# Every seventh chunk of expert weights multiplied whole as fp32

## The chip, the cores and the metric

The kernel runs on one core of one Trainium2 chip. The metric is the device time of one launch in microseconds (us). In the profile PE is TensorE's matmul, PEld its weight load, DVE is VectorE, ACT is ScalarE, POOL is GpSimd and SP is SyncE, which issues most DMAs.

## The reference

A block of 256 tokens of width 1024 goes through a mixer, a memory attention, a mixture of experts and then two further attention and feed-forward layers, all in fp32. The change lies in the mixture of experts, which is, cut to its core:

```
expert = grp * EXPERTS_PER_GROUP + top_i          # 2 of 32 experts for each of 256 tokens
def run_block(args):
    e, tok, w = args
    xb = xt[tok]
    hid = jax.nn.silu(xb @ w_gate[e]) * (xb @ w_up[e])     # 1024 x 512 each
    return (hid @ w_down[e]) * w[:, None].astype(xb.dtype) # 512 x 1024
```

All 32 experts' weights are read: 32 x 6 MB of fp32.

## The kernel before

Matmuls are done in fp32r, which keeps fewer bits of an fp32 number. To stay near fp32, each operand is split into a high half (the value rounded to fp32r) and a low half (what is left), and the halves' products are added up.

**The experts.** The 32 experts go in 16 units of two. Each expert's tokens sit in 32 slots. The stationary operand is built so that a 128-column slice of it (`xf[:, k0 + k, e * 64:e * 64 + P]`) holds the high and the low half of one expert's tokens, with zeros in the other expert's place, so one matmul with it gives high and low rows of the result at once; a small matmul with `comb` adds them up later.

**The chunks.** The weights come in chunks of 256 rows by 512 columns (128 partitions x 2 x 512, 512 KB), 12 for an expert, 384 in all. For each chunk in turn `stream` (L1021) does: one DMA on SP's queue into a raw buffer (`load`, L276); `high` (L286) on ACT, which writes the high half `wh`; `low` (L291) on DVE, which subtracts it from the raw chunk and writes the low half `wl` (for a few early chunks on POOL, `POOLED`); and `go` in `parts` (L1010), which issues four matmuls of 128x512 on PE: two row blocks of `wh`, then two of `wl`. Then `tick` runs whatever the agenda has due at this chunk: `clock[0]` is the number of chunks done. There are 4 buffers for `wh`, 4 for `wl`, and 27 places for raw chunks (`places`, `shared`), so ACT and DVE can be up to four chunks ahead of PE.

**The order.** Every instruction of this path is wrapped in `keep`, which fixes its order on its engine. Unit u runs `up(u)` (16 chunks for gate and up), then `down(u - 1)` (8 chunks). So chunk numbers run: up(0) 0 to 15, up(1) 16 to 31, down(0) 32 to 39, up(2) 40 to 55, and so on, 24 for each unit. Between chunks stand, by the agenda:
- `read` and `hidden` of `up` (L1067, L1072): after the third chunk of the following down, ACT copies the sums (L1068) and PE adds high and low rows with `comb` (L1070); after the fifth chunk, `hidden` runs a chain ACT sigmoid (L1078), DVE, DVE, ACT cast (L1082), DVE. ACT and DVE work in order, so the sixth chunk's `high` stands behind that chain.
- `scatter` (L1106), `gather` (L933) and `weights` (L1046): small fp32 matmuls and transposes; an fp32 matmul shows as two records in the trace.

The matmuls of `mm<-` are those of up, those of `at<-` are of down.

Of the kernel before, what the change touches and what calls it, by code (L numbers as in the profile page):

```python
# [13 lines left out]
F32 = mybir.dt.float32  # L14
# [6 lines left out]
P = 128  # L21
# [4 lines left out]
KC = 2  # L26
RAW = 4
MOE_RAW = 16
LAG = 3
POOLED = (4, 24, 3)  # L30
EARLY = 25
PAST = 16
OVER = 10
# [81 lines left out]
def forward(ctx: ExitStack, tc: tile.TileContext, a: dict, out: bass.AP):  # L115
    nc = tc.nc
    mm = nc.tensor.matmul
# [151 lines left out]
    def keep(ins):  # L269
        return tc.keep_in_program_order(ins)  # L270

    def chunk(pool, tag, kc, n, dt=F32):
        v = new(pool, [P, KC, 512], dt, name=tag, **({"bufs": 2} if tag == "Y" else {}))
        return v if n == 512 else v.rearrange("p k n -> p (k n)")[:, 0:kc * n].rearrange("p (k n) -> p k n", n=n)

    def load(parts, kc, n, pool=wraw, tag="raw"):  # L276

        raw = chunk(pool, tag, kc, n)
        at = 0
        for src in parts:  # L280
            w = src.shape[1]
            nc.sync.dma_start(out=raw[:, :kc, at:at + w], in_=src.rearrange("(k p) n -> p k n", p=P))
            at += w
        return raw

    def high(raw, kc, n, order=free):  # L286
        h = chunk(whi, "wh", kc, n, F32R)
        order(nc.scalar.activation(h[:, :kc], raw[:, :kc], AF.Copy))  # L288
        return h

    def low(raw, h, kc, n, order=free, eng=nc.vector):  # L291
        l = chunk(wlo, "wl", kc, n, F32R)
        order(eng.tensor_sub(l[:, :kc], raw[:, :kc], h[:, :kc].bitcast(F32)))  # L293
        return l
# [422 lines left out]
    def nextraw():  # L717

        return next(v for v in raws if not closing or v[0] is not big or v[1] in ("kTc", "vc"))
# [169 lines left out]
    last = len(UNITS) - 1  # L889
    xs2 = []  # L890
    for u in range(2):
        xs2.append(new(mp, [P, KD, 3, 2, 32], F32R, name="xs%d" % u))
        if u == 0:
            wt = s3("wt", 32)
            upcoming = [W[e, k0 * P:(k0 + KC) * P] for i in range(2) for e in UNITS[i] for W in (wg, wu) for k0 in range(0, KD, KC)]
            ahead.extend(load([src], KC, 512, *nextraw()) for src in upcoming[len(first):][:EARLY])
    hs2 = []
# [7 lines left out]
    agenda, clock = collections.defaultdict(list), [0]  # L905
# [7 lines left out]
    def tick():  # L913
        clock[0] += 1
        for fn, args in agenda.pop(clock[0], ()):
            fn(*args)
# [93 lines left out]
    def parts(xf, e, nk, last, acc, W, col):  # L1010

        def go(k0, ww):
            for i in range(2):
                for k in range(KC):
                    keep(mm(acc, xf[:, k0 + k, e * 64:e * 64 + P], ww[i][:, k],  # L1015
                            start=(e == 0 and k0 == 0 and i == 0 and k == 0),
                            stop=(e == last and k0 + KC == nk and i == 1 and k == KC - 1)))

        return [(W[k0 * P:(k0 + KC) * P, col:col + 512], functools.partial(go, k0)) for k0 in range(0, nk, KC)]

    def stream(chunks):  # L1021
        for src, go in chunks:
            if ready:
                go(ready.popleft())
            else:
                raw = ahead.popleft() if ahead else load([src], KC, 512, *nextraw())
                h = high(raw, KC, 512, keep)
                go((h, low(raw, h, KC, 512, keep, nc.gpsimd if clock[0] < POOLED[1] and clock[0] % POOLED[0] == POOLED[2] else nc.vector)))
            tick()

    def flat(v):
# [27 lines left out]
    def up(u):  # L1059

        G, U = new(psm, [P, 512], name="mm"), new(psm, [P, 512], name="mm")
        at(2 if u else PAST, weights, u)
        stream(up_chunks(u, G, U))
        gu = [new(tmp, [P, 512], name="rows") for _ in range(2)]
        ps = new(psm, [P, 2, 4, 64], name="mm")

        def read(i, v):  # L1067
            keep(nc.scalar.copy(gu[i], v))  # L1068
            for k in range(4):
                keep(mm(ps[:, i, k], gu[i][:, k * P:(k + 1) * P], comb, start=True, stop=True))  # L1070

        def hidden():  # L1072
            if u < 2:
                hs2.append(new(mp, [P, 4, 3, 2, 32], F32R, name="hs%d" % u))
                nc.gpsimd.memset(hs2[u][:, :, 1].bitcast(F32), 0.0)
            hs = hs2[u % 2]
            hid = new(mp2, [P, 4, 64], name="hid")
            keep(nc.scalar.activation(hid, ps[:, 0], AF.Sigmoid))  # L1078
            keep(nc.vector.tensor_mul(hid, hid, ps[:, 0]))
            keep(nc.vector.tensor_mul(hid, hid, ps[:, 1]))  # L1080
            hv = hid.rearrange("p k (e r) -> p k e r", e=2)
            keep(nc.scalar.copy(hs[:, :, 0::2, 0], hv))  # L1082
            keep(tt(hs[:, :, 0::2, 1], hv, hs[:, :, 0::2, 0].bitcast(F32), op=ALU.subtract))

        at(LAG - 4, read, 0, G)
        at(LAG, read, 1, U)
        at(LAG + 2, hidden)
# [5 lines left out]
    def down(u):  # L1093

        Y = [new(psa, [P, 512], name="at") for _ in range(2)]
        stream(down_chunks(u, Y))
        Yg[u] = new(mp, [P, 2, 512], name="Y", bufs=2)
        for half in range(2):
            at(LAG - 2 + 2 * half, lambda *v: keep(nc.scalar.copy(*v)), Yg[u][:, half], Y[half])
# [125 lines left out]
    for i, v in enumerate(both):  # L1225
        at(ADDS + i, add, *v, last - 1)
    chunks = down_chunks(last, Y)
    stream([chunks[i] for i in (0, 1, 4, 5, 2, 3, 6, 7)])
    flush()
    rows_out(0)  # L1230
# [323 lines left out]
```

## Time and profile before

| what | value |
|---|---|
| time, median of 3 runs | 1588.86 us (1588.35 to 1589.14) |
| the profiled execution's own time | 1591.64 us |
| its span | 1590.0 us |
| PE busy, share of the span | 1532.9 us, 96% |
| DVE busy | 1190.1 us, 75% |
| ACT busy | 992.1 us, 62% |
| mean granted TensorE clock | 0.989 of full |

The experts' chunks are multiplied from 296 us to 826 us of the span. The profiled execution is 2.8 us above the median of the timed runs, 1.64 us of its time lies outside the span. Busy time of PE counts modelled ends that overlap with the next matmul, so PE's load is better read from the distances between starts.

### The profile page before, as it was taken

The page shows a single profiled execution, that of the slowest core. Times are in us where ns is not written, and L with a number is a line of the kernel's source. Part 1 is how long each engine was busy: PE and PEld are TensorE (multiplying, and loading weights), DVE is VectorE, ACT ScalarE, POOL GpSimd, SP SyncE. Part 2 cuts the span into 40 slices and gives each one's busy share as a digit, 9 for nine tenths or more (in the row PEclk, how much of TensorE's full clock was granted, in tenths as well). Part 3 has the DMA queues.
Part 4 walks back from the last instruction along what each step waited for, and adds up shares of the span by engine and source line. Part 5 has one row for each costly group of instructions (what it writes and reads, how often), then busy time and mean ns, then how long its engine had stood idle before and what let it go on. Part 6 is the DMA issues. An engine that isn't in the chain of part 4 may idle for free. (4 is left out here: it accounts for less than half of the span.)

```text
span 1590.0 us, 20604 instructions
## 1 busy us (share of the span) xinstructions
PE 1532.9 (96%) x7099; PEld 1194.5 (75%) x7099; DVE 1190.1 (75%) x1498; ACT 992.1 (62%) x1353; POOL 199.8 (13%) x95
## 2 busy tenths in 40 slices
PE   7999999699999999999999999999999999999998
PEld 5778887466776767767667887888888887888886
DVE  5665575789999999999887876766656876766654
ACT  5455554579878887797774666555544566455543
POOL 1110000434335141142001000000000000000000
PEclk9999999899999999999999999999999999999999
DMA  8645559689999999999956545566567545566653
GB/s 283 218 137 160 182 173 375 209 295 370 386 387 387 386 387 340 341 386 386 387 187 195 147 141 164 182 189 186 185 186 220 168 137 152 178 195 186 184 187 106
DMA packets 220348, 383.59 MB, mean 241 GB/s; under 512 B 13464, under 2 KB 60000, under 8 KB 219856
## 3 DMA queue, kind: packets, MB, share of 16 engines
q1 hardware_dynamic: 217584, 373.76, 70.2%
q0 software_dynamic: 1648, 6.84, 1.4%
q10 hardware_dynamic: 1008, 1.64, 0.3%
q8 instruction: 57, 0.93, 0.2%
q14 instruction: 51, 0.42, 0.1%
HBM read 381.10 MB, written 2.65 MB: 241 GB/s over the span
## 5 line engine op out<-in xcount | busy, mean ns | idle before, releaser
L293 DVE TENSOR_TENSOR wl<-raw,wh 128x1024 fp32r<-128x1024 f32 x599 | 718.0, 1227 | 239.6 <-ACT wh L288 226.1
L288 ACT ACTIVATE wh<-raw 128x1024 fp32r<-128x1024 f32 x606 | 624.0, 1057 | 303.2 <-PE mm L327 258.9
L1015 PE MATMUL mm<-wl,xs 128*128 128x512 f32 x512 | 186.4, 446 | 8.6 <-DVE wl L293 5.5
L1039 POOL TENSOR_TENSOR selw<-sel,wt 128x128 f32<-128x128 f32 x32 | 139.7, 4385 | 272.9 <-DVE sel L925 187.6
L1015 PE MATMUL mm<-wh,xs 128*128 128x512 f32 x512 | 164.0, 403 | 0.6 <-ACT wh L288 0.6
L1015 PEld LDWEIGHTS mm<-wl,xs 128*128 128x128 f32 x512 | 91.3, 192 | 66.2 <-DVE wl L293 32.8
L327 PE MATMUL mm<-wh,hAl 128*128 128x512 f32 x424 | 139.1, 409 | 0.0
L327 PE MATMUL mm<-wh,hAh 128*128 128x512 f32 x424 | 134.3, 397 | 2.7 <-ACT wh L288 2.7
L327 PE MATMUL mm<-wl,hAh 128*128 128x512 f32 x424 | 134.3, 398 | 0.0
L327 PE MATMUL mm<-wl,hBh 128*128 128x512 f32 x424 | 133.3, 394 | 0.0
L327 PE MATMUL mm<-wh,hBl 128*128 128x512 f32 x424 | 132.4, 393 | 0.1
L327 PE MATMUL mm<-wh,hBh 128*128 128x512 f32 x424 | 132.1, 393 | 0.0
L1015 PEld LDWEIGHTS mm<-wh,xs 128*128 128x128 f32 x512 | 97.0, 191 | 27.2 <-ACT wh L288 3.7
L1015 PE MATMUL at<-wl,hs 128*128 128x512 f32 x256 | 89.4, 430 | 7.9 <-DVE wl L293 7.9
L327 PEld LDWEIGHTS mm<-wh,hAh 128*128 128x128 f32 x424 | 79.3, 190 | 19.8 <-ACT wh L288 3.1
L1015 PE MATMUL at<-wh,hs 128*128 128x512 f32 x256 | 87.2, 422 | 5.4 <-ACT wh L288 5.3
L327 PEld LDWEIGHTS mm<-wl,hAh 128*128 128x128 f32 x424 | 79.4, 190 | 17.2
L327 PEld LDWEIGHTS mm<-wh,hBh 128*128 128x128 f32 x424 | 78.9, 188 | 17.6
L327 PEld LDWEIGHTS mm<-wh,hBl 128*128 128x128 f32 x424 | 78.5, 188 | 18.0 <-issue 1.4
L327 PEld LDWEIGHTS mm<-wl,hBh 128*128 128x128 f32 x424 | 78.5, 188 | 16.9 <-issue 0.3
L327 PEld LDWEIGHTS mm<-wh,hAl 128*128 128x128 f32 x424 | 75.3, 191 | 12.3 <-issue 0.8
L1015 PEld LDWEIGHTS at<-wl,hs 128*128 128x128 f32 x256 | 45.1, 188 | 34.9 <-DVE wl L293 21.9
(482 smaller groups left out, 2245.5 us busy)
## 6 DMA issues: line engine op xcount, KB each, us to landing
raw<-in_w_in_dram SPq DMA_DIRECT2D x121, 512.0 KB, 3.7
raw<-in_w_exp_down_dram SPq DMA_DIRECT2D x101, 512.0 KB, 10.8
raw<-in_w_exp_gate_dram SPq DMA_DIRECT2D x95, 512.0 KB, 10.8
raw<-in_w_exp_up_dram SPq DMA_DIRECT2D x93, 512.0 KB, 10.8
raw<-in_w_ffn_in_dram SPq DMA_DIRECT2D x176, 256.0 KB, 3.2
raw<-in_w_ffn_out_dram SPq DMA_DIRECT2D x44, 512.0 KB, 3.8
raw<-in_w_out_dram SPq DMA_DIRECT2D x24, 512.0 KB, 3.8
raw<-in_w_ckv_dram SPq DMA_DIRECT2D x8, 512.0 KB, 3.9
```

Source lines behind the costliest of these rows:

```text
L288: order(nc.scalar.activation(h[:, :kc], raw[:, :kc], AF.Copy))
L293: order(eng.tensor_sub(l[:, :kc], raw[:, :kc], h[:, :kc].bitcast(F32)))
L327: order(mm(ps[t][:, :n], xs[k0 + k][part][:, t * P:(t + 1) * P], ww[:, k, :n], start=(k0 == 0 and i == 0 and k == 0), stop=(k0 + kc == nk ...
L1015: keep(mm(acc, xf[:, k0 + k, e * 64:e * 64 + P], ww[i][:, k], start=(e == 0 and k0 == 0 and i == 0 and k == 0), stop=(e == last and k0 + K ...
L1039: nc.gpsimd.tensor_tensor(selw[:, :, :, d], sel, wt[:, :, 2 * u:2 * u + 2].rearrange("p t (e o) -> p t e o", o=1).to_broadcast([P, NT, 2, ...
```

## The change

From chunk 25 on, each chunk whose number leaves 5 when divided by 7 (26, 33, 40, ... 383: 52 chunks) is not split. It is multiplied as plain fp32 straight from its raw buffer, and the stationary slice is read as fp32 too: two matmuls of 128x512 fp32 instead of four of fp32r. No `high`, no `low`, and the raw buffer is given back by PE and no more by DVE.

```
+WHOLE = (7, 5)
...
         def go(k0, ww):
-            for i in range(2):
+            for i, w in enumerate(ww):
+                rows = xf if len(ww) == 2 else xf.bitcast(F32)
                 for k in range(KC):
-                    keep(mm(acc, xf[:, k0 + k, e * 64:e * 64 + P], ww[i][:, k],
+                    keep(mm(acc, rows[:, k0 + k, e * 64:e * 64 + P], w[:, k],
                             start=(e == 0 and k0 == 0 and i == 0 and k == 0),
-                            stop=(e == last and k0 + KC == nk and i == 1 and k == KC - 1)))
+                            stop=(e == last and k0 + KC == nk and i == len(ww) - 1 and k == KC - 1)))
...
                 raw = ahead.popleft() if ahead else load([src], KC, 512, *nextraw())
-                h = high(raw, KC, 512, keep)
-                go((h, low(raw, h, KC, 512, keep, nc.gpsimd if clock[0] < POOLED[1] and clock[0] % POOLED[0] == POOLED[2] else nc.vector)))
+                if clock[0] % WHOLE[0] == WHOLE[1] and clock[0] > POOLED[1]:
+
+                    go((raw,))
+                else:
+                    h = high(raw, KC, 512, keep)
+                    go((h, low(raw, h, KC, 512, keep, nc.gpsimd if clock[0] < POOLED[1] and clock[0] % POOLED[0] == POOLED[2] else nc.vector)))
```

On PE, in down(3) of the kernel before, from the fourth chunk (107) on: each chunk is a pair of rows, `wh` and `wl`, and the comb matmuls stand ahead of the fourth.

```order
L1070 MATMUL mm<-c_ones,rows 128x64 x4
L1015 MATMUL at<-wh,hs_2913 128x512 x2
L1015 MATMUL at<-wl,hs_2913 128x512 x2
L1015 MATMUL at<-wh,hs_2913 128x512 x2
L1015 MATMUL at<-wl,hs_2913 128x512 x2
L1015 MATMUL at<-wh,hs_2913 128x512 x2
L1015 MATMUL at<-wl,hs_2913 128x512 x2
L1015 MATMUL at<-wh,hs_2913 128x512 x2
L1015 MATMUL at<-wl,hs_2913 128x512 x2
```

The same place on PE in the changed kernel (lines are 2 to 6 further down there):

```order
L1076 MATMUL mm<-c_ones,rows 128x64 x4
L1017 MATMUL at<-wh,hs_2901 128x512 x2
L1017 MATMUL at<-wl,hs_2901 128x512 x2
L1017 MATMUL at<-wh,hs_2901 128x512 x2
L1017 MATMUL at<-wl,hs_2901 128x512 x2
L1112 MATMUL tp<-Y,selT 128x512
L1017 MATMUL at<-wh,hs_2901 128x512 x2
L1017 MATMUL at<-wl,hs_2901 128x512 x2
L1017 MATMUL at<-raw,hs_2901 128x512 x2
```

Chunk 110 has become one row of two fp32 matmuls from `raw`, and a scatter matmul, whose order is not fixed by `keep`, has moved ahead of chunk 109.

On ACT at the same place, before: the copy of the sums, the `high` of chunks 107 and 108, the chain of `hidden`, and the `high` of chunks 109 (from `gain`), 110, 111 and 112.

```order
L1068 COPY rows<-mm 128x512
L288 ACTIVATE wh<-raw 128x1024 x2
L1078 ACTIVATE hid<-mm 128x256
L1082 CAST hs_2706<-hid 128x4x2x32
L288 ACTIVATE wh<-gain 128x1024
L288 ACTIVATE wh<-raw 128x1024 x3
L1099 COPY Y<-at 128x512
```

And on ACT in the changed kernel:

```order
L1074 COPY rows<-mm 128x512
L289 ACTIVATE wh<-raw 128x1024 x2
L1084 ACTIVATE hid<-mm 128x256
L1088 CAST hs_2706<-hid 128x4x2x32
L289 ACTIVATE wh<-gain 128x1024
L289 ACTIVATE wh<-raw 128x1024 x2
L1105 COPY Y<-at 128x512
```

One `high` is gone behind the chain; the chain itself stands where it stood, between the `high` of the fifth and of the sixth chunk.

## Rows read from the trace of the kernel before

**Rows 1.** Busy us by stretch: PE, PEld, DVE, ACT, POOL, clock, DMA share, GB/s.
```profile
460.00:500.00 40.00, 39.40 (x182) 29.47 (x180) 38.52 (x42) 33.33 (x42) 13.42 (x3) 1.00 1.05 386
```

**Rows 2.** Timeline in an up phase: start, length, engine, operation, count.
```profile
498.95 6.89 DVE L293 TENSOR_TENSOR wl<-raw,wh 128x1024 fp32r<-128x1024 f32 x6
...
501.36 0.73 PE L1015 MATMUL mm<-wl,xs 128*128 128x512 f32 x2
...
502.49 0.73 PE L1015 MATMUL mm<-wl,xs 128*128 128x512 f32 x2
```

**Rows 3.** Timeline: matmuls of several kinds with no wait between them.
```profile
783.49 0.63 PE L1015 MATMUL mm<-wl,xs 128*128 128x512 f32 x2
...
783.96 0.63 PE L1015 MATMUL mm<-wh,xs 128*128 128x512 f32 x2
...
826.33 1.88 PE L1131 MATMUL mm<-Y,selT 128*128 128x512 f32 x4
...
479.46 2.00 PE L933 MATMUL tp<-sel,xr 128*128 128x128 f32 x16
```

**Rows 4.** Expert chunks' matmuls by stretch: PE, PEld busy (count), clock, DMA share, GB/s.
```profile
354.40:826.60 472.20, 389.33 (x1393) 250.74 (x1391) 1.00 0.99 363
```

**Rows 5.** PE's other groups in the same stretch: count, busy time, mean ns.
```profile
L1106 PE MATMUL tp<-Y,selT 128*128 128x512 f32 x112 | 56.2, 592 | 0.4 <-PEq L1138 0.4
L1070 PE MATMUL mm<-c_ones,rows 128*128 128x64 f32 x224 | 28.0, 268 | 0.0
L933 PE MATMUL tp<-sel,xr 128*128 128x128 f32 x192 | 23.7, 277 | 0.0
L1046 PE MATMUL mm<-c_ident,selw 128*128 128x128 f32 x28 | 6.1, 271 | 0.0
L1131 PE MATMUL mm<-Y,selT 128*128 128x512 f32 x9 | 4.7, 592 | 0.0
L1119 PE MATMUL tp<-xr,c_ones 1*128 1x512 f32 x8 | 4.5, 640 | 0.0
L1131 PE MATMUL mm<-x,c_ident 128*128 128x512 f32 x8 | 4.1, 598 | 0.0
```

**Rows 6.** Timeline in down(3), around the chain of hidden (chunks 107 to 109).
```profile
445.05 1.00 PE L1070 MATMUL mm<-c_ones,rows 128*128 128x64 f32 x8
446.09 0.39 ACT L1078 ACTIVATE hid<-mm 128x256 f32<-128x256 f32 x1 [1.99 <-PE mm L1070]
...
446.87 0.62 PE L1015 MATMUL at<-wh,hs 128*128 128x512 f32 x2
...
447.33 0.62 PE L1015 MATMUL at<-wl,hs 128*128 128x512 f32 x2
...
448.83 0.73 PE L1015 MATMUL at<-wh,hs 128*128 128x512 f32 x2 [0.88 <-ACT wh L288]
...
450.09 0.73 PE L1015 MATMUL at<-wl,hs 128*128 128x512 f32 x2 [0.52 <-DVE wl L293]
```

**Rows 7.** The same place one unit later, timeline.
```profile
484.23 0.63 PE L1015 MATMUL at<-wh,hs 128*128 128x512 f32 x2
...
485.46 0.72 PE L1015 MATMUL at<-wl,hs 128*128 128x512 f32 x2 [0.60 <-DVE wl L293]
```

**Rows 8.** PE's waits, 340 to 827 us: total, times, longest.
```profile
PE at L1015 <- DVE wl L293: 7.9, 14, 0.6
PE at L1015 <- ACT wh L288: 5.3, 6, 0.9
PE mm L1015 <- DVE wl L293: 2.1, 1, 2.1
```

**Rows 9.** The view of rows 1, behind the one long wait of an up phase.
```profile
748.80:752.30 3.50, 3.48 (x8) 2.79 (x9) 3.50 (x3) 2.37 (x3) 1.56 (x2) 0.51 1.05 387
```

**Rows 10.** Timeline of SP's queue: the last expert loads are issued.
```profile
784.21 11.46 SPq L282 DMA_DIRECT2D raw<-in_w_exp_down_dram  x9
```

**Rows 11.** DMA issues by line: count, size, median us from issue to landing.
```profile
raw<-in_w_exp_down_dram SPq DMA_DIRECT2D x101, 512.0 KB, 10.8
```

## The prediction

> **What bounds the kernel now.** I read the busy times by stretch first. In the expert stage they leave no engine plainly ahead: PE, DVE and the DMA queues are all nearly full in [rows 1]. So the question is which one the others wait for, and what each has to spare.
>
> The timeline of an up phase answers the first half. DVE makes six lows in 6.89 us, 1.148 us a chunk, with no gap; PE's second pairs start 1.13 us apart [rows 2]. DVE sets the pace there, and PE waits a little in every chunk. In the down phases the waits look different: PE stops for a whole microsecond behind the chain of `hidden` [rows 6, 7], and the list of waits counts 7.9 us for lows and 5.3 us for highs at those matmuls [rows 8].
>
> The second half, what PE has to spare, I take from distances between starts. A pair of fp32r matmuls starts 0.467 us after the pair before in an up phase [rows 3] and 0.46 us in a down phase [rows 6], so one takes 0.2335 or 0.23, on the mix 0.2325. A 512-column fp32 record takes (1.88 - 0.592) / 3 = 0.429 us, from four records in a row [rows 3] and the length of one [rows 5]. A `comb` record takes about (1.00 - 0.268) / 7 = 0.105, of which I use 0.101 because the next matmul starts early; a 128-column record (2.00 - 0.277) / 15 = 0.115 [rows 3, 5, 6]. From chunk 36 to the end there are 472.2 us and in them 1393 records of the chunks [rows 4], 137 other 512-column records, 224 of `comb`, and 220 of 128 columns [rows 5]. That is 323.9 + 58.8 + 22.6 + 25.3 = 430.6 us of PE work. PE is idle for 41.6 us of 472.2, and this is all that a faster DVE could give back to it.
>
> DMA is no limit yet. The last nine loads are issued from 784.21 to 795.67 us [rows 10] and a load lands 10.8 us after its issue [rows 11], so the last one lands at about 806.5, some 20 us before the last chunk is multiplied at 826.
>
> **What the change removes.** 52 lows of 1.148 us, 59.7 us of DVE, and 52 highs of ACT. With six of seven chunks split, DVE needs 6.9 us for seven chunks in place of 8.0.
>
> **What it adds.** A whole chunk is two fp32 matmuls, four records, 4 x 0.429 = 1.716 us, where four fp32r records took 4 x 0.2325 = 0.93. That is 0.786 us more of PE for each, 39.3 us for the 50 whole chunks from chunk 36 on. The scatter and the sum over x are fp32 matmuls of the same shape [rows 5], and they stand between fp32r matmuls now, so I see no reason for another price. PE then has 430.6 + 39.3 = 469.9 us of work in a stretch of 472.2. **The bound moves from DVE to PE**, and the best that can come of it, with PE never waiting, is -2.3 us. Chunks 26 and 33 lie in an earlier stretch, where DVE sets the pace too; I count them as nothing (1.6 us of PE work against waits of about that size, between -1 and +1).
>
> The price may be weighed against the Trainium skill: its page "FP8 and Floating Point Precision", section "TensorE Precision Notes", says that true fp32 takes four passes through the array. By that rule, as an estimate, a whole chunk would be 2 x 4 x 0.2325 = 1.86 us and the sum 7 us higher; the rows have 1.716, a little under four passes, and I go by the rows.
>
> **Which of PE's waits stay.** PE's 41.6 us of idle time are of two sorts. The small ones, 0.1 us at each pair of an up phase, come from DVE's pace, and they go. The large ones come from the chain of `hidden`, which is a latency and no load. ACT waits for `comb` until 446.0, the chain follows, and only then comes the high of the sixth chunk of the down phase. PE has two finished chunks to cover that time and stops. The distance 447.33 to 448.83 is 1.50 for a pair of 0.46, so 1.04 is lost, and 448.83 to 450.09 loses another 0.80: 1.84 us [rows 6]. One unit later gather matmuls cover part of it, and 1.23 - 0.46 = 0.77 us is lost [rows 7]. The waits count 14 for lows and 6 for highs [rows 8], which is seven of the large kind, chunks 61, 109, 157 and so on in steps of 48, and seven of the small kind, chunks 38, 86, 134 and so on.
>
> The change doesn't touch the chain; the order on ACT shows it at its old place. A large gap goes only where a whole chunk happens to stand at it. Chunk numbers that leave 5 on division by 7 decide this:
> - Large: 61 is itself whole, the gap goes. 301 and 349 have a whole chunk among the two ahead, which covers 0.79 more. At 109 and at 301 a scatter matmul (two records, 0.86) now stands ahead of the waiting one. At 253 the wait is short already, about 1.0. What stays is 0 + 0.98 + 1.84 + 1.84 + 1.0 + 0.2 + 1.05 = 6.9 us.
> - Small: at 134, 182, 230 and 278 a whole chunk covers it. At 38, 86 and 326 it stays: 2.3 us.
>
> **After a gap DVE has no lead.** Until the next whole chunk, PE takes 0.93 us a chunk and DVE 1.148, so PE still waits 0.21 us in each. Behind the gaps that stay, 23 split chunks come before the next whole one, up to 4.8 us. `comb` and scatter matmuls stand between some of them, so I take half, 2.4.
>
> **The one long wait** of an up phase, 2.1 us [rows 8], is followed by 3.5 us at a granted clock of 0.51, the lower of the two levels (1.2 GHz), in which eight records pass that take 1.87 at full clock [rows 9]. Chunk 327, just ahead of it, becomes whole and gives DVE a lead, so I expect most of this to go, and 0.3 to stay; at the branch of the overflow code I leave 0.5.
>
> **The sum.** -2.3 + 6.9 + 2.3 + 2.4 + 0.8 = +10.1 us. The profiled execution had 1591.64 us of its own time, so its like would be 1601.7; on the median of the runs, 2.8 lower, 1588.86 + 10.1 = 1599.0. What follows the experts is PE's work in a chain behind the last chunk, so I expect the delay to pass through whole.
>
> **The rivals.** Differences within 0.2% (3.2 us) are about what a measurement of this kernel can't tell from no change.
> - *PE fills every gap.* With DVE at 85% of its former load, leads could be long enough that all waits vanish: -2.3 us, 1586.6, no measurable change. For it: PE runs without a wait through several chunks around 783 us, where scatter work sits between the chunks [rows 3]. Against it: the chain, where DVE and ACT are idle themselves while PE waits. Chance 0.2, with everything that ends within 0.2%.
> - *Faster: DVE's pace was the price and PE has room.* If a whole chunk cost PE no more than DVE's 1.148 us, seven chunks would take PE 6 x 0.93 + 1.15 + 2.1 (other work, 106.7 / 348 a chunk) = 8.8 us where they take 472.2 / 348 x 7 = 9.5 now. The queue of loads would then end it: last landing at 806.5, some 5 us of work behind it, 812 in place of 826, 14 us less, 1575. The point from which it decides is 1.3 us for a whole chunk, below which PE keeps room for the gaps. For it: PE's price is for other operands than these. Against it: three groups of fp32 matmuls of this shape, all with 592 or 640 ns [rows 5]. Chance 0.1.
> - *All gaps stay.* If no whole chunk covers a gap, 18.3 us stay for 9.2, and 4.8 for 2.4: +21.6, 1610. Chance 0.1, within slower.
> - *Loads come late*, since PE gives a whole raw buffer back some chunks later than DVE did. 48 chunks of 0.524 MB at 386 GB/s [rows 1] take 65.2 us, PE with its gaps 482.3 / 348 x 48 = 66.5, and loads have a lead of 20 us: a few us at most, chance 0.03, within slower.
>
> **How the numbers follow.** Slower by over 0.2%: 0.7, of which 0.57 for the sum as it stands. Same 0.2, faster 0.1. The range goes from 1586, PE without gaps, to 1608, most gaps kept; below it lies the faster case, above it the worst of the slower. The likeliest case alone spans 1594 to 1604.
>
> **What the profile after would show.** Records of `mm<-raw` or `at<-raw` of about 592 ns, 0.429 apart, four for a chunk: right in price. PE's waits for lows in up phases nearly gone, DVE idle between lows and waiting for PE or ACT, and the gaps at 157 and 205 still there: right in mechanism. A last chunk multiplied at about 836 us in place of 826. Wrong if whole chunks take under 1.3 us, if PE's summed idle time falls to under 5 us, or if SP waits for PE while highs wait for DMA.

## The result and the profile after

The changed kernel takes 1602.87 us (1602.32 to 1603.17, 4 runs) against 1588.83 for the kernel before. The ratio is 1.0093 with an interval of 1.0081 to 1.0106: 14.0 us slower, where 10.1 had been predicted.

The busy times by stretch, in the columns of [rows 1], show what moved. DVE has gone from 38.5 us of 40 to 32.7, and DMA moves 357 GB/s in place of 386. PE is at 40.00 after 39.40; since ends of matmuls are modelled, this says little, and the balance below is the better measure of PE.

```profile
460.00:500.00 40.00, 40.00 (x171) 28.08 (x170) 32.66 (x36) 27.71 (x36) 4.43 (x4) 1.00 0.99 357
```

The timeline shows a whole chunk's price directly: four fp32 records from `raw` between pairs of fp32r ones, which answer to [rows 3].

```profile
797.68 0.63 PE L1017 MATMUL mm<-wh,xs 128*128 128x512 f32 x2
798.15 0.63 PE L1017 MATMUL mm<-wl,xs 128*128 128x512 f32 x2
798.62 1.88 PE L1017 MATMUL mm<-raw,xs 128*128 128x512 f32 x4
799.93 1.03 PE L1017 MATMUL mm<-wh,xs 128*128 128x512 f32 x2
800.80 0.63 PE L1017 MATMUL mm<-wl,xs 128*128 128x512 f32 x2
```

From 798.62, four records, then a pair of `wh`, and at 800.80 the next pair of `wl`: 2.18 us for four fp32 records and one pair. Less the 0.467 of that pair, 1.71 us is left for the whole chunk, as predicted from [rows 3, 5]. It is so throughout the stage: from the first to the fourth record of a whole chunk it is 1.287 us by the median of the 48 that stand in one piece (1.285 to 1.343), 0.429 a record.

The groups of PE's instructions between chunk 36 and the end of the stage show that records of whole chunks have the length of the scatter's, 592 to 595 ns, in up and in down phases.

```profile
L1112 PE MATMUL tp<-Y,selT 128*128 128x512 f32 x112 | 56.0, 593 | 0.9 <-ACT Y L1105 0.5 <-PEq L1144 0.4
L1017 PE MATMUL mm<-raw,xs 128*128 128x512 f32 x96 | 45.3, 592 | 0.0
...
L1017 PE MATMUL at<-raw,hs 128*128 128x512 f32 x56 | 26.5, 595 | 0.0
```

The list of PE's waits in the stage answers to [rows 8]. Waits for lows in down phases have gone from 14 to 7, for highs from 6 to 2, and the long one in an up phase from 2.1 us to 0.8.

```profile
PE at L1017 <- DVE wl L294: 3.8, 7, 0.6
PE at L1017 <- ACT wh L289: 1.8, 2, 0.9
PE mm L1017 <- DVE wl L294: 0.8, 1, 0.8
PE tp L1112 <- ACT Y L1105: 0.5, 1, 0.5
PE tp L1112 <- PEq L1144: 0.4, 1, 0.4
```

The two waits for highs are at chunks 157 and 205, two of the places where the prediction left the gap whole. The timeline of down(5) around chunk 157 repeats [rows 6] almost to the hundredth: `comb`, the chain of `hidden` on ACT and DVE, then the high, then the low. DVE had been idle for 1.78 us before the chain, so this gap isn't a matter of its load.

```profile
513.45 1.00 PE L1076 MATMUL mm<-c_ones,rows 128*128 128x64 f32 x8
514.26 0.70 PE L1017 MATMUL at<-wh,hs 128*128 128x512 f32 x2
514.49 0.39 ACT L1084 ACTIVATE hid<-mm 128x256 f32<-128x256 f32 x1 [2.81 <-PE mm L1076]
...
514.91 0.42 DVE L1085 TENSOR_TENSOR hid<-hid,mm 128x256 f32<-128x256 f32 x1 [1.78 <-ACT hid L1084]
...
517.23 0.73 PE L1017 MATMUL at<-wh,hs 128*128 128x512 f32 x2 [0.88 <-ACT wh L289]
...
518.49 0.73 PE L1017 MATMUL at<-wl,hs 128*128 128x512 f32 x2 [0.52 <-DVE wl L294]
```

At chunk 61, which is itself whole, PE goes from one chunk to the next without a stop, and the gap is gone:

```profile
383.15 0.62 PE L1017 MATMUL at<-wl,hs 128*128 128x512 f32 x2
383.61 1.88 PE L1017 MATMUL at<-raw,hs 128*128 128x512 f32 x4
384.92 1.02 PE L1017 MATMUL at<-wh,hs 128*128 128x512 f32 x2
```

**A balance of the stage.** For every kernel below I made the same sum as the prediction did, over all matmul records from the first of chunk 36 to the end of the stage: the distance between starts beyond a record's own time is idle time of PE. A record's own time is the prediction's, so "work" counts records at those prices, and only the length of the stage is measured apart from them. For the kernel before this gives 472.1 us of stage, 430.0 of work and 42.1 idle (the prediction had 41.6). For the changed kernel it gives 487.7, 469.1 and 18.6. Work has grown by 39.1 us, idle time has shrunk by 23.4, and the stage is 15.6 us longer.

The two profiled executions differ by less, 11.5 us in their own times. The one of before had two stretches of 3.4 us at a granted clock of 0.50 outside this part of the stage (254 and 851 us), in which 8 and 10 records pass where the changed kernel's execution has 20 and 17 at 1.00. The medians of the runs are the better measure.

### The profile page after: what moved, and what is told of

The parts are those of the page before. It is cut to its first block, busy times and chain, and to the rows that moved or that the text cites. A ratio compares the mean times of both kernels' runs of the same rounds, so it can differ in the third digit from the quotient of the medians.

```text
span 1601.4 us, 20399 instructions
## 1 busy us (share of the span) xinstructions
PE 1554.5 (97%) x7099; PEld 1197.1 (75%) x7099; DVE 1141.1 (71%) x1446; ACT 946.3 (59%) x1301; POOL 97.0 (6%) x95
## 5 line engine op out<-in xcount | busy, mean ns | idle before, releaser
L294 DVE TENSOR_TENSOR wl<-raw,wh 128x1024 fp32r<-128x1024 f32 x560 | 679.7, 1235 | 258.2 <-ACT wh L289 243.2
L289 ACT ACTIVATE wh<-raw 128x1024 fp32r<-128x1024 f32 x567 | 586.1, 1057 | 310.1 <-PE mm L328 256.8
L1017 PE MATMUL mm<-wl,xs 128*128 128x512 f32 x446 | 154.0, 427 | 8.0 <-DVE wl L294 4.2
L1017 PE MATMUL mm<-wh,xs 128*128 128x512 f32 x446 | 160.0, 440 | 0.6 <-ACT wh L289 0.6
L1017 PEld LDWEIGHTS mm<-wl,xs 128*128 128x128 f32 x446 | 83.3, 191 | 43.6 <-DVE wl L294 10.9
L1017 PEld LDWEIGHTS mm<-wh,xs 128*128 128x128 f32 x446 | 83.6, 191 | 39.7 <-issue 20.4
L1017 PE MATMUL at<-wh,hs 128*128 128x512 f32 x218 | 79.4, 445 | 1.9 <-ACT wh L289 1.8
L1017 PE MATMUL at<-wl,hs 128*128 128x512 f32 x218 | 74.2, 422 | 3.9 <-DVE wl L294 3.8
L1045 POOL TENSOR_TENSOR selw<-sel,wt 128x128 f32<-128x128 f32 x32 | 38.4, 1220 | 387.3 <-DVE sel L926 269.4
L1112 PE MATMUL tp<-Y,selT 128*128 128x512 f32 x112 | 56.0, 593 | 0.9 <-ACT Y L1105 0.5
## 6 DMA issues: line engine op xcount, KB each, us to landing
raw<-in_w_exp_gate_dram SPq DMA_DIRECT2D x95, 512.0 KB, 10.4
raw<-in_w_exp_up_dram SPq DMA_DIRECT2D x93, 512.0 KB, 10.7
```

Of the source, the lines that this page charges most:

```text
L1017: keep(mm(acc, rows[:, k0 + k, e * 64:e * 64 + P], w[:, k], start=(e == 0 and k0 == 0 and i == 0 and k == 0), stop=(e == last and k0 + KC ...
L1045: nc.gpsimd.tensor_tensor(selw[:, :, :, d], sel, wt[:, :, 2 * u:2 * u + 2].rearrange("p t (e o) -> p t e o", o=1).to_broadcast([P, NT, 2, ...
L1112: mm(ps, sT[u][:, t * P:(t + 1) * P], Yg[u][:, half], start=(i == 0), stop=(i == len(units) - 1))
```

## The experiments

The theory: after the change PE is the bound, a whole chunk costs PE 0.786 us, and it pays only what PE had been waiting for at that place. The rivals: the loss comes from something else than PE's price (raw buffers given back late, the new order); the cost is simply in proportion to the number of whole chunks; DVE's 59.7 us of relief are worth much more than this.

**gaps_only.** Whole are only the chunks at the seven large gaps.

```
-WHOLE = (7, 5)
+WHOLE = (48, 13)
```

> Only chunks 61, 109, 157, 205, 253, 301 and 349 are whole, which are the sixth chunks of the down phases whose large gap the chain of hidden makes. If PE's price and the gaps decide (my theory): 7 x 0.786 = +5.5 us of PE work, and seven gaps of 1.73 us (one of 1.0) go, -11.4 us: about -6 us, 1583. If a whole chunk is a cost in proportion to its number (rival: 14.0 us for 52): 7 x 0.27 = +2 us.

Measured: 1580.46 us against 1588.2, ratio 0.9957 (0.9944 to 0.997), 7.7 us faster. A second measurement of the same kernel, together with the last two below:

> The kernel of gaps_only once more, for a comparison on the same chip: -7.7 us against the kernel before, as measured.

It gave 1583.01 against 1588.57, ratio 0.9965 (0.9953 to 0.9977), 5.6 us faster. So whole chunks that cost 14 us as 52 spread evenly gain 6 to 8 us as seven that stand where PE waits. That it is the place and not only the small number, gaps_and_lead below shows with chunks at other places. The timeline at chunk 109 shows the place: where the kernel before loses 1.84 us [rows 6], PE now goes through four records of `gain`. The next low still makes it wait a little, since the chain is as long as it was.

```profile
441.16 0.62 PE L1017 MATMUL at<-wl,hs 128*128 128x512 f32 x2
441.62 1.88 PE L1017 MATMUL at<-gain,hs 128*128 128x512 f32 x4
442.93 1.02 PE L1017 MATMUL at<-wh,hs 128*128 128x512 f32 x2
443.92 0.73 PE L1017 MATMUL at<-wl,hs 128*128 128x512 f32 x2
```

Stage 465.7 us, work 435.6, idle 30.1: 12.0 us less idle for 5.5 more work.

**price_only.** The change as it is, but the halves are made all the same.

```
                 if clock[0] % WHOLE[0] == WHOLE[1] and clock[0] > POOLED[1]:
+                    low(raw, high(raw, KC, 512, keep), KC, 512, keep)
                     go((raw,))
```

> The 52 whole chunks are multiplied whole, but their high and low halves are made all the same and not used. This leaves the price on PE and takes the relief of DVE and ACT away. If PE is the bound after the change and DVE's relief only removes PE's waits: PE has 40.9 us more work, DVE has 1.148 us for every chunk as before while PE takes 1.337 on the mean, so most of the small waits go all the same, and the large gaps at whole chunks come back: +15 to +24 us over the kernel before. If the relief of DVE is worth its 59.7 us of busy time (rival), taking it away costs far more: over +40 us.

Measured: 1609.25 us, ratio 1.013 (1.0116 to 1.0145), 21.0 us slower than before and 7 slower than the change. Without any relief idle time falls from 42.1 to 25.0 all the same, because PE is slower; the relief takes it on to 18.6. The 59.7 us taken from DVE, with the highs taken from ACT, are worth some 7 us here. DVE is at 37.1 of 40, nearly as full as in the kernel before:

```profile
460.00:500.00 40.00, 40.00 (x175) 28.67 (x174) 37.12 (x40) 31.10 (x40) 5.15 (x3) 1.00 0.99 364
```

**relief_only.** No halves for the 52 chunks, and PE repeats the chunk before; the 52 chunks' own weights are left out of the result.

```
+    before_it = [None]
...
-                    go((raw,))
+                    go(before_it[0])
                 else:
                     h = high(raw, KC, 512, keep)
-                    go((h, low(raw, h, KC, 512, keep, nc.gpsimd if clock[0] < POOLED[1] and clock[0] % POOLED[0] == POOLED[2] else nc.vector)))
+                    before_it[0] = (h, low(raw, h, KC, 512, keep, nc.gpsimd if clock[0] < POOLED[1] and clock[0] % POOLED[0] == POOLED[2] else nc.vector))
+                    go(before_it[0])
```

> For the 52 chunks no halves are made, and PE multiplies the halves of the chunk before once more, four fp32r matmuls as in the kernel before: DVE and ACT are relieved, PE pays nothing. These chunks' own weights are left out of the result. My theory: PE's idle time falls as in the changed kernel, from 42 to about 19 us, and nothing is added: -23 us by PE alone, but the loads then end the stage (last landing about 806, some 5 us behind it, 812 in place of 826.5): -12 to -20 us. If the change was slower for another reason than PE's price (buffers given back late, order): still no gain, -3 to +14 us.

Measured: 1577.11 us, ratio 0.993 (0.9915 to 0.9944), 11.1 us faster, just short of the 12 to 20 expected. The sign is the theory's, but the reason given for the size was not right: idle time fell to 30.7 us only, and it was not the loads that ended the gain, for the last nine are issued from 773.82 us on and the last chunk is multiplied at 810. Its list of waits shows why. The waits in down phases are nearly all there, and a new one of 3.0 us has come at the branch of the overflow code:

```profile
PE at L1017 <- DVE wl L294: 6.1, 11, 0.6
PE at L1017 <- ACT wh L289: 4.4, 5, 0.9
...
PE tp L1114 <- PEq L1146: 3.0, 1, 3.0
```

A whole chunk covers a gap by the time that PE itself takes for it. Without that time the relief does not reach the gaps. So the loss of the change is PE's price: with the price and without the relief +21.0, with the relief and without the price -11.1. (The new order of the scatter matmuls was not tested by itself.) The two add up to +9.9 against +14.0, since under the price there is less idle time left for the relief to remove.

**half_dose** and **double_dose.** 26 and 103 whole chunks.

```
-WHOLE = (7, 5)
+WHOLE = (14, 5)
```

> Every fourteenth chunk whole, 26 of them. My theory: +20.4 us of PE work; the large gap at 61 goes, 301 in part, the small ones at 134 and 230, 4.1 us in all, and some 12 us of the small waits that come from DVE's pace: about +4 us, 1593. A cost in proportion to the number (rival): +7 us.

```
-                if clock[0] % WHOLE[0] == WHOLE[1] and clock[0] > POOLED[1]:
+                if clock[0] % WHOLE[0] in (1, 5) and clock[0] > POOLED[1]:
```

> Whole chunks at two residues, 1 and 5 of 7: 103 of them. My theory: with PE the bound, each further whole chunk costs its full 0.786 us, less what little idle time is left: 81 us of PE work, idle time down from 42 to some 11: +50 us, 1638. A cost in proportion to the number, 0.27 us each as in the change (rival): +28 us. If DVE's relief paid more with each chunk (rival): under +28 us.

Measured: 1594.74 us, ratio 1.0041 (1.0027 to 1.0056), +6.5 us, and 1630.3 against 1588.92, ratio 1.0269 (1.0253 to 1.0285), +41.4 us. The half dose doesn't tell the theories apart: 6.5 lies nearer the rival's 7 than my 4. The double dose does, though it stayed below my +50: the second 51 whole chunks cost 27.4 us, twice as much as the first 52. A cost in proportion would have stopped at +28. Idle time fell to 6.5 us, where I had expected 11. DVE is busy for 27 of 40 us there:

```profile
460.00:500.00 40.00, 40.00 (x167) 27.06 (x166) 27.24 (x31) 21.34 (x29) 2.59 (x2) 1.00 0.93 336
```

**gaps_and_lead** and **gaps_and_two.** The seven of gaps_only, chunk 327, and one or two more chunks in the up phases that follow.

```
-                if clock[0] % WHOLE[0] == WHOLE[1] and clock[0] > POOLED[1]:
+                if (clock[0] % WHOLE[0] in (13, 17) or clock[0] == 327) and clock[0] > POOLED[1]:
```

In gaps_and_two it is `in (13, 17, 22)`.

> Whole are the seven chunks of gaps_only, the fourth chunk after each of these (65, 113, 161 and so on, in the up phase that follows, to give DVE a lead there) and chunk 327 ahead of the one long wait. My theory: -7.7 us as in gaps_only, a further 7 x (0.79 - 1.6) = -6, and -2 for the long wait and the half clock behind it: about -15 us, 1573. If the loads end the stage (rival): no more than -10. If whole chunks pay only at the gaps themselves (rival): -7.7 + 6.3 = about -1 us.

> As gaps_and_lead, with one more whole chunk in each of these up phases (70, 118, 166 and so on). My theory: the lead of the first lasts for most of the phase, so the second costs 7 x 0.79 and brings little: 2 to 5 us slower than gaps_and_lead. If DVE's pace were still the bound there (rival): faster than gaps_and_lead.

Measured: 1587.27 us, ratio 0.9993 (0.9984 to 1.0002), and 1592.5, ratio 1.0028 (1.0017 to 1.0038). The first missed by 14 us and came out at the rival's -1: the added chunks were a cost. I had put them into the wrong up phases. Taken by twelve chunks, idle time of gaps_only is 0.1 us in chunks 72 to 83, where the scatter of two units fills PE, and 1.0 and 1.6 in chunks 84 to 107, in the other kind of up phase. With a whole chunk at 65, chunks 60 to 83 take 35.08 us where they took 34.29 in gaps_only: 0.79 more, the full price, with idle time as it was. (A scatter matmul has also moved from the first half of these chunks to the second.) The second of gaps_and_two costs the same again, 5.2 us by the medians.

**gaps_both** and **gaps_both_lead.** So the next two put whole chunks before and into the other kind of up phase.

```
-                if clock[0] % WHOLE[0] == WHOLE[1] and clock[0] > POOLED[1]:
+                if (clock[0] % WHOLE[0] in (13, 37) or clock[0] == 327) and POOLED[1] < clock[0] < 372:
```

In gaps_both_lead it is `in (13, 37, 45)`.

> Whole are the seven chunks of gaps_only, the sixth chunks of the other down phases (37, 85, 133, ... 325), and chunk 327: 15 in all. In the profile of gaps_only PE's idle time of 30 us lies ahead of and in the up phases behind those other down phases, 36 to 60, 84 to 108 and so on, some 3.4 us in each, and hardly any in the up phases behind the first ones, where scatter work fills PE. My theory, that a whole chunk pays where PE waits and costs 0.786 us where it does not: each of the seven covers 0.76 and gives DVE a lead worth about 1.1: -1.1 us net each, chunk 327 -1.3: 8 to 9 us under gaps_only, about 1572. If whole chunks pay only at the large gaps (rival): no better than gaps_only, or up to 5 us slower.

> As gaps_both, with one more whole chunk in each up phase behind the second kind (45, 93, 141 and so on), the phase in which DVE sets the pace: 22 whole chunks. My theory: up to 1.5 us of small waits are left in each of these phases, against 0.786 of price: 3 to 5 us under gaps_both, if the loads do not end the stage before. If the lead of the first lasts (rival): 3 to 6 us over gaps_both.

Measured: 1580.58 us against 1588.57, ratio 0.9958 (0.9944 to 0.9971), and 1578.46, ratio 0.9943 (0.9929 to 0.9957). gaps_both is 2.4 us under the gaps_only of the same chip, not 8 to 9. Outside the branch of the overflow code its idle time fell by 10 us for 6.3 of work, but it lost some 4 at the branch, where PE waits 3.1 us in place of 0.4 and the granted clock is 0.50 for 3.4 us behind it. The wait list of gaps_both_lead has a wait at the same place:

```profile
PE tp L1112 <- PEq L1144: 2.9, 1, 2.9
PE tp L1248 <- DVE xg L1243: 1.8, 1, 1.8
PE mm L1017 <- DVE wl L294: 1.0, 1, 1.0
```

No wait for a high or a low in a down phase is left there. gaps_both_lead gained a further 2.1 us by the medians (3 to 5 expected): chunks 48 to 59 have 0.19 us of idle time where they had 1.30 in gaps_both. These steps of 2 us are small against the scatter of the runs, whose times overlap; in the profiled executions the stage takes about 465 us in the second measurement of gaps_only, 465.4 and 462.3, so only the last step shows there. gaps_both_lead has the lowest median of the kernels that compute the whole result: 22 whole chunks, 10.1 us under the kernel before, where the change is 14.0 over it. Its idle time is 15.0 us.

**The whole set in one table**, by the sum over the stage from chunk 36 on; the last column is the difference of the medians.

| kernel | stage, us | PE's work | PE idle | against before |
|---|---|---|---|---|
| before | 472.1 | 430.0 | 42.1 | |
| changed | 487.7 | 469.1 | 18.6 | +14.0 |
| price_only | 494.1 | 469.1 | 25.0 | +21.0 |
| relief_only | 460.7 | 430.0 | 30.7 | -11.1 |
| half_dose | 476.6 | 449.5 | 27.1 | +6.5 |
| double_dose | 515.1 | 508.6 | 6.5 | +41.4 |
| gaps_only | 465.7 | 435.6 | 30.1 | -7.7, -5.6 |
| gaps_and_lead | 469.4 | 441.7 | 27.7 | -1.7 |
| gaps_and_two | 475.0 | 447.4 | 27.6 | +3.6 |
| gaps_both | 465.4 | 442.0 | 23.4 | -8.0 |
| gaps_both_lead | 462.3 | 447.3 | 15.0 | -10.1 |

The column of work counts each whole chunk at 0.78 us; what was measured is the stage and the median.

## Why the prediction was right

**The bound moves from DVE to PE.** Right, and shown: PE is idle for 18.6 of 487.7 us, and giving DVE its work back costs 7 us, not 59.7.

**The price, 0.786 us a whole chunk.** Right: the trace has 1.71 us for a whole chunk and 0.429 for a record of it, where 1.716 and 0.429 were predicted. The Trainium skill, page "FP8 and Floating Point Precision", section "TensorE Precision Notes", has four passes for true fp32. The estimate from it, at 0.2325 a pass, was 1.86 us a chunk, where the trace has 1.71; the measurement decides.

**Which gaps stay.** Right in kind and nearly in place. At 61 the gap is gone, at 157 and 205 it is whole (1.73 us each by the sum over records, predicted 1.84). At 109, 253 and 349 there is about 0.9, of which 0.69 in one wait (predicted 0.98, 1.0 and 1.05), at 301 nothing above 0.25 (0.2). Of the small kind 86 and 326 are left with 0.76, as predicted, and 38 is not; there a scatter matmul waits 0.6 in its place. All waits above 0.25 us make 9.3 us, with 0.97 near chunk 330 and 0.6 at the branch; the prediction's terms for these add up to 10.0.

**The one long wait.** Right in part: 0.97 us of it stay, where 0.3 was predicted. The stretch at the lower clock behind it is gone, the granted clock is 1.00 through the whole stage.

**After a gap DVE has no lead: the term that was too small.** 2.4 us were predicted for all small waits; those of up to 0.25 us add up to 9.4. The wrong step was "the small ones ... come from DVE's pace, and they go". The ones at chunks of an up phase did go, from 11.5 us to 0.7 by the same sum. The others did not, since not all of them come from DVE's pace. In double_dose, where DVE is busy for 27 of 40 us, small waits still make 5.2 us, and chunks 336 to 347 have 1.4 idle in the kernel before and 1.4 in double_dose. The traces show what this is made of: 3.4 us stand at the same places in every kernel. Such a place are the four matmuls of `to_all`, two records each, which spread a row over all partitions:

```profile
773.17 0.63 PE L1017 MATMUL mm<-wl,xs 128*128 128x512 f32 x2
773.73 1.12 PE L1125 MATMUL tp<-xr,c_ones 1*128 1x512 f32 x2
774.78 0.73 PE L1017 MATMUL mm<-wh,xs 128*128 128x512 f32 x2
775.35 0.63 PE L1017 MATMUL mm<-wl,xs 128*128 128x512 f32 x2
```

From 773.17 to 775.35 it is 2.18 us for two fp32r pairs and two records of `tp<-xr`, which is 0.39 more than 2 x 0.467 and 2 x 0.429. Four such places make 1.6 us, and the first pairs behind the `comb` matmuls another 1.8. The balance calls this idle time, but it is the same in every kernel here, whatever DVE was relieved of. Most of the rest, 3.8 us, stands at chunks of down phases, where there were 3.6 before; why it stays there was not tested.

**The sum.** It came to +10.1 and the stage shows +15.6. The small waits, 7.0 us too few, account for the difference; the larger ones were 0.7 too many, and the finer sum finds 0.5 more idle time in the kernel before. Of +15.6 the medians show +14.0; what makes the 1.6 between them is open. The last chunk is multiplied at 840.31 us, where about 836 was predicted.

**The rivals.** PE did not fill every gap, and no whole chunk cost under 1.3 us. Loads are issued later, as the fourth rival has it: SP waits 70.7 us for chunks' matmuls on PE in the stage, where it is 0.4 us in the kernel before. But that this costs time is excluded for this kernel: neither PE nor a high on ACT waits for a load in the stage, and the last nine expert loads are issued from 794.43 us on, while the last chunk is multiplied at 840.31:

```profile
794.43 9.29 SPq L283 DMA_DIRECT2D raw<-in_w_exp_down_dram  x9
```

At 10.4 to 10.7 us from issue to landing they are there some 25 us ahead, more than before.

## What to carry to other kernels

When three engines are near full, relief of the one that sets the pace is worth only the idle time of the next one, here 42 us of PE against 60 us taken from DVE, and much of that idle time may be a latency that no relief reaches. Before moving work, add up the next engine's own work from distances between starts and list its waits by place. Whole chunks cost 14 us as 52 at a fixed step and gain 10 us as 22 that stand at the waits or just ahead of the stretches with waits.

## What the hardware showed that was not expected

**GpSimd's `selw` products run slow beside DVE's lows.** In the kernel before, 32 of them take 398 ns to 19 us each, 4385 ns on the mean. In the changed kernel the longest is 5.2 us and the mean 1220 ns; in price_only, where DVE has all its lows, the longest is 20 us again. The rows are those of the tile `selw` in the three kernels, in this order; the times are minimum, median and maximum in ns.

```profile
L1039 POOL TENSOR_TENSOR selw<-sel,wt x32: 398/1141/19038, 317.7 to 749.0; 128x128 f32<-128x128 f32 x32
```

```profile
L1045 POOL TENSOR_TENSOR selw<-sel,wt x32: 396/1320/5203, 315.6 to 764.4; 128x128 f32<-128x128 f32 x32
```

```profile
L1045 POOL TENSOR_TENSOR selw<-sel,wt x32: 392/1253/20035, 315.5 to 768.4; 128x128 f32<-128x128 f32 x32
```

A long one ends when DVE's row of lows does. In the kernel before, two products from 427.70 us on are through at 447.08, 0.6 us behind the last of a row of lows that began before them and had no gap:

```profile
427.70 19.38 POOL L1039 TENSOR_TENSOR selw<-sel,wt 128x128 f32<-128x128 f32 x2 [13.25 <-PE mm L1046]
441.84 4.62 DVE L293 TENSOR_TENSOR wl<-raw,wh 128x1024 fp32r<-128x1024 f32 x4
446.51 0.42 DVE L1079 TENSOR_TENSOR hid<-hid,mm 128x256 f32<-128x256 f32 x1
```

In price_only two products from 430.63 on are through at 448.77, and the row of lows ends at 448.15. In gaps_both, where only 15 chunks have no low, the longest product takes 4.7 us, so the number of lows alone doesn't decide it.

The Trainium skill, page "SBUF — State Buffer", section "Who interferes with whom", says that a DVE instruction with two SBUF inputs contends with a GpSimd instruction that reads SBUF. The trace agrees as far as these rows go, a low having the inputs `raw` and `wh`; no run here took the port by itself.

**The branch of the overflow code** costs PE 0.4 us in most kernels, 0.9 in gaps_only and 2.9 to 3.1 in relief_only, gaps_both and gaps_both_lead. (In gaps_both the list puts the wait down to a low and not to PE's sequencer; the scatter matmul that waits needs no low.) In gaps_both and gaps_both_lead the granted clock is 0.50 behind it for 3.4 us, the lower level (1.2 GHz); in relief_only, after a wait as long, it stays at 1.00. What makes the wait longer there was not tried and stays open.
